# Hybrid decoder block on one core: transfers in program order during attention, weights asked for eight half pieces ahead and in the order of their use

## The chip, the cores and the metric

The kernel runs on one core of a Trainium2 chip. The metric is the device time of one execution in microseconds (us). Five instruction streams work side by side, each strictly in its own order: TensorE (PE, matrix products), VectorE (DVE), ScalarE (ACT), GpSimd (POOL), and SyncE (SP), which here only issues transfers (DMAs). They wait for one another through semaphores. A TensorE clock of 1.00 in the profile is the full 2.4 GHz level; the other level is 1.2 GHz, and a stretch between them is a mean.

## The reference, cut to what matters

One decoder layer on 512 tokens of width 1024, all in float32. Two attention mixers share one normalised input; their gated sum goes through an output projection, and a gated feed-forward of width 2816 follows.

```
proj = rmsnorm(x) @ w_in                       # 1024 -> 4808 columns, split into
qa,ka,va (8 heads of 64), qb (8 heads), kb,vb (one shared head), qi,ki,wi (indexer), ga,gb (gates)
y_a = dilated window attention(rope(qa), rope(ka), va)      # three masks, merged by log-sum-exp
score = sum_h wi_h * relu(rope(qi)_h . rope(ki))            # 512 x 512, causal
y_b = attention(rope(qb), rope(kb), vb) over the 128 best keys of each row of score
x = x + (sigmoid(ga) * (y_a @ w_up_a) + sigmoid(gb) * (y_b @ w_up_b)) @ w_out
x = x + (silu(h @ w_gate) * (h @ w_up)) @ w_down ;  out = rmsnorm(x)
```

## The kernel before

**Products.** Every float32 operand is split in two parts, `hi` (rounded) and `lo` (the rest), and `mm3` makes one product of three matmuls: L201 (hi with hi), L202 and L203 (the two cross terms). Which of L202 and L203 uses the weight's `lo` depends on the side the weights stand on.

**Weights.** A `Chunk` is a block of weight columns, mostly 256 wide, fetched in pieces. `fetch` (L153) asks for one piece by a DMA from SP into one of 5 `raw` buffers. `more` does one half piece at a time: the first call makes `whi` on ACT (L172), and fetches first if nothing was fetched; the second makes `wlo` (L164) on POOL or DVE: in turns before attention, all on POOL during it. There are 8 buffers each for `whi` and `wlo`, that is two chunks of four pieces. If a matmul asks for a piece that isn't there, `Chunk.__getitem__` calls `more` on the spot. `ahead()` takes one half piece of the first unfinished chunk in the list `coming`. It is called 8 times (`LEAD`) before the attention steps. Inside `run_part` it stands behind `if MAN[0]`, and `MAN[0]` is never set, as `DV` is 0. So all later weights are asked for on the spot in the program's text.

**Order of the work.** The kernel is written against a scheduler. Engines in a `manual_schedule` take their instructions in program order; the others get their order at build time from priorities (`level`: attention steps 2, other parts 3, top-k 4), readiness and free buffers, which can move a weight's fetch and split far ahead of its place in the text. Once built, every engine's order is fixed. From L838 to `pe_order.close()`, which is the stage of interest, only PE is manual. Behind it no engine is.

**The stage of interest** in the order of PE's program:
1. Indexer queries and keys are turned (`heads_T`, `idx`), while `P0` makes queries and keys of the first head pair ("slot" products, weights from `qka_parts(0)`). After each slot product `rope_T` copies the result (ACT L488, `raw`), swaps its halves by four DMAs on SP (L491, `sw<-raw`, 64 KB each), and DVE multiplies and adds (L495, L498, L499); then ACT, DVE and POOL make `hi` and `lo` of queries and keys (L422, L426, L441, L442, L446, L447).
2. Scores of the indexer: 24 products (`dots`), each followed by a ReLU on ACT (L861) and a weighted sum on DVE (L866). Between them stand the last half of `P0` and `V0`, the value products of head pairs 0 and 1 ("proj", eight parts; its four pieces are the first chunk of kind `128x2x256`). `V0` isn't in `coming`.
3. 36 attention steps `attn_step(t)`. Step t makes the score products of two heads (`sc`), their softmax (L678 on DVE, exponential L679 on ACT, L683 on DVE, L684 on POOL), and turns the probabilities of the step before (`pT`, L693, L697, L698); every fourth step multiplies by the values (`y`). Between steps, parts of other products are run from a queue: P1, P2 and P3 (head pairs 1 to 3), G0, G1, ... (gates), B (queries and keys of the second mixer), V1. Each part is six matmuls of 512 columns or twelve of 256.
4. The 128 best keys of each score row: 16 rounds of `max` and 15 of `match_replace` (L629, L634) for each of three row blocks, then 18 instructions (L640 to L647) that make the mask. They go to DVE at the lowest priority, and the second mixer needs their result from step 16 on.

The list `order` names the chunks that `ahead()` takes: w1, w2, w3 (of P1 to P3), wkv and wq (of B), wv1 (of V1), wg_ (gates), then those of `w_up_a`.

Of the kernel before, what the change touches and what calls it, by code (L numbers as in the profile page):

```python
# [38 lines left out]
def hybrid_block(ctx: ExitStack, tc: tile.TileContext, x, norm_mix, w_in, w_up_a, w_up_b, w_out,  # L39
# [90 lines left out]
    MAN = [False]  # L130
# [58 lines left out]
    def ahead():  # L189

        while coming and coming[0].done():
            coming.pop(0)
        if coming:
            coming[0].more()
# [142 lines left out]
    def settle(n=1):  # L337
        for _ in range(n):
            for e in later:
                e[0] -= 1  # L340
            while any(e[0] <= 0 for e in later):
                i = next(i for i, e in enumerate(later) if e[0] <= 0)
                later.pop(i)[1]()

    def run_part():
        cost, part = queue.pop(0)
        part()
        settle()
        if MAN[0]:
            ahead()  # L350
        topk_some(TK[2])
        debt[0] -= cost

    def fill(us):

        debt[0] += us
        with level(3):
            while queue and debt[0] > 0:
                run_part()
        if not queue:  # L360
            debt[0] = min(debt[0], 0.0)

    def drain(until=0):
        with level(3):
            while len(queue) > until:
                run_part()
            if not queue:
                settle(9)
        debt[0] = 0.0
# [182 lines left out]
    def va_parts(c):  # L552

        get_w = stream(win, [(VA + 256 * c, 256)])

        def done(p_, b):
            for pr in (2 * c, 2 * c + 1):
                if b == 0:
                    va[pr] = ap.tile([P, NB, 2, P], F32R, tag="va", bufs=VAB, name=f"va{pr}")
                src = p_[:, pr % 2 * P:(pr % 2 + 1) * P].rearrange("p (s d) -> p s d", s=2)  # L560
                vh, vl = va[pr][:, b, :, 0:64], va[pr][:, b, :, 64:128]
                nc.scalar.activation(vh, src, AF.Copy, scale=rs1[:, b:b + 1])
                defer(1, lambda vl=vl, src=src, vh=vh: nc.vector.scalar_tensor_tensor(  # L563
                    vl, src, rs1[:, b:b + 1], vh.bitcast(F32), op0=ALU.mult, op1=ALU.subtract))
        return [proj_parts(get_w, 256, b, lambda p_, b=b: done(p_, b)) for b in range(NB)], get_w
# [11 lines left out]
    def gate_parts(base, c, store):  # L577

        get_w = stream(win, [(base + c * 256, 256)])

        def part(m, k0, p_):
            if k0 == 0:
                p_.append(acc("gate"))
            W = get_w()
            for k in range(k0, k0 + 2):
                l = (W[k][0][:, m * P:(m + 1) * P], W[k][1][:, m * P:(m + 1) * P])
                mm3(p_[0], l, hT[k], k == 0, k == KT - 1)
            if k0 + 2 == KT:
                t = k2(name="gate")
                nc.vector.tensor_tensor(t, p_[0], rb1[0], op=ALU.mult)  # L590
                defer(1, lambda: nc.scalar.activation(t, t, AF.Tanh, scale=0.5))
                store.append(t)
        res = []
        for m in range(2):
            p_ = []
            res.append([(6 * 512 / 2400, lambda m=m, k0=k0, p_=p_: part(m, k0, p_)) for k0 in range(0, KT, 2)])
        return res, get_w

    def flat(*lists):
        return [x for l in lists for x in l]  # L600
# [51 lines left out]
    def topk_some(n):  # L652
        with level(TKL):
            for _ in range(n):
                if topk and next(topk[0], None) is None:
                    topk.clear()
# [179 lines left out]
        weights(2, 8)  # L836
    start.close()
    pe_order = ExitStack()  # L838
    pe_order.enter_context(tc.manual_schedule(engines={mybir.EngineType.PE}))
    nc.sync.dma_start(ropeT, c_ropeT)  # L840
    queue += flat(*second[:NSB])
    drain()
# [38 lines left out]
    V1, wv1 = va_parts(1)  # L881
    B, TV, (*wq, wkv) = mqa_parts(bT)
    G, wg_ = zip(*[gate_parts(base, c, store) for base, store in ((GA, mA), (GB, mB)) for c in range(4)])
# [1 line left out]
    for i, at in enumerate(GAT):  # L885
        seq[at] = seq[at] + flat(*G[i])
    queue += flat(*seq)
    order = [c() for c in (w1, w2, w3, wkv, wv1, *wq, *wg_)]
    for g in G[len(GAT):]:
        queue += flat(*g)  # L890
    yS = []
# [218 lines left out]
```

## Time and profile before

| what | value |
|---|---|
| median of 3 runs (lowest, highest) | 775.24 us (775.01, 775.41) |
| the profiled execution, its own time | 774.55 us |
| its span, first to last instruction | 772.8 us |
| PE busy, share of the span | 744.1 us, 96% |
| DVE, ACT, POOL busy | 435.6, 352.6, 281.4 us |
| mean TensorE clock | 0.993 |
| HBM traffic | 91 GB/s over the span |

Between the span and the time of the profiled execution lie 1.75 us that the trace doesn't show. All other times are read from that one execution, and are counted from the start of the span. A busy PE is not PE at its peak, since matmuls overlap: a 512-column matmul lasts 0.39 us in the trace, but the next begins some 0.23 us after it.

### The profile page before, as it was taken

To read this page: it belongs to the slowest core of one execution; us is meant where nothing else is said; L and a number is where in the kernel's file an instruction comes from. 1 tells how busy PE (TensorE), PEld (TensorE's weight loads), DVE (VectorE), ACT (ScalarE), POOL (GpSimd) and SP (SyncE) were. 2 spreads that over 40 slices of the span, in tenths; PEclk is the share of its full clock that TensorE was granted. 3 is DMA by queue.
4 is the path that set the end of the run, shared out by engine and by line. 5 is a ranking of instruction groups with operands and counts; after the bars stand their busy time and mean duration, and the time that the engine had idled before them with its cause. 6 is when DMAs were issued, how large, how long until landed. Compare 5 with 4: busy or idle time off the path is not lost.

```text
span 772.8 us, 10634 instructions
## 1 busy us (share of the span) xinstructions
PE 744.1 (96%) x3621; PEld 625.2 (81%) x3621; DVE 435.6 (56%) x910; ACT 352.6 (46%) x722; POOL 281.4 (36%) x263
## 2 busy tenths in 40 slices
PE   8988998988999999999999999999999999999995
PEld 7977887886888888888887888888888888888884
DVE  5789989997766557765334344344433343222235
ACT  7366566655666667533425333333333333121233
POOL 2653656645545455422121222222222222222223
PEclk9999999999999999999999999999999999999999
DMA  8352433322432221533232332233223333323202
GB/s 278 80 137 54 102 91 88 89 76 69 117 88 70 73 66 55 176 112 107 82 106 59 109 103 88 83 109 109 84 85 105 109 101 90 105 86 109 83 14 109
DMA packets 68502, 74.53 MB, mean 96 GB/s; under 512 B 5392, under 2 KB 55584, under 8 KB 68448
## 3 DMA queue, kind: packets, MB, share of 16 engines
q1 hardware_dynamic: 68448, 73.86, 32.7%
q8 instruction: 28, 0.46, 0.2%
q14 instruction: 26, 0.21, 0.1%
HBM read 68.46 MB, written 2.10 MB: 91 GB/s over the span
## 4 chain that ended last, share of the span: by engine, by line
PE 82%; DVE 10%; ACT 3%; issue 2%; DMA 1%; SPq 0%; POOL 0%; ACTq 0%; DVEq 0%; POOLq 0%
PE o L202 5%; PE u L203 5%; PE o L203 5%; PE u L202 5%; PE u L201 5%; PE o L201 5%; PE g L203 5%; PE g L202 5%; PE g L201 5%; PE gate L201 3%; PE gate L202 3%; PE gate L203 3%; PE x L203 2%; PE x L201 2%; PE x L202 2%
## 5 line engine op out<-in xcount | busy, mean ns | idle before, releaser
L164 POOL TENSOR_TENSOR wlo<-raw,whi 128x512 fp32r<-128x512 f32 (+1 forms) x156 | 206.1, 1331 | 386.6 <-ACT whi L172 376.4
L172 ACT ACTIVATE whi<-raw 128x512 fp32r<-128x512 f32 (+1 forms) x242 | 149.6, 625 | 240.1 <-PE u L203 70.9
L164 DVE TENSOR_TENSOR wlo<-raw,whi 128x512 fp32r<-128x512 f32 x86 | 71.9, 836 | 128.3 <-ACT whi L172 127.8
L201 PE MATMUL g<-h2h,whi 128*128 128x512 f32 x176 | 68.7, 390 | 0.0
L203 PE MATMUL g<-h2l,whi 128*128 128x512 f32 x176 | 68.7, 390 | 0.0
L202 PE MATMUL g<-h2h,wlo 128*128 128x512 f32 x176 | 68.6, 390 | 0.0
L201 PE MATMUL u<-h2h,whi 128*128 128x512 f32 x176 | 68.5, 389 | 0.0
L202 PE MATMUL u<-h2h,wlo 128*128 128x512 f32 x176 | 68.5, 389 | 0.0
L203 PE MATMUL u<-h2l,whi 128*128 128x512 f32 x176 | 68.5, 389 | 0.0
L201 PE MATMUL o<-whi,ah 128*128 128x512 f32 x176 | 68.5, 389 | 0.0
L202 PE MATMUL o<-whi,al 128*128 128x512 f32 x176 | 68.5, 389 | 0.0
L203 PE MATMUL o<-wlo,ah 128*128 128x512 f32 x176 | 68.5, 389 | 0.0
L684 POOL TENSOR_SCALAR sm<-sm,st 128x256 f32<-128x256 f32 (+3 forms) x64 | 40.0, 632 | 62.4 <-DVE st L683 52.1
L201 PE MATMUL gate<-hTh,whi 128*128 128x512 f32 x128 | 51.6, 403 | 0.0
L203 PE MATMUL gate<-hTl,whi 128*128 128x512 f32 x128 | 50.2, 392 | 0.0
L202 PE MATMUL gate<-hTh,wlo 128*128 128x512 f32 x128 | 50.1, 391 | 0.0
L679 ACT ACTIVATE sm<-sm,st 128x256 f32<-128x256 f32 (+3 forms) x64 | 35.6, 557 | 23.3 <-DVE st L678 23.1
L1025 DVE TENSOR_TENSOR u<-u,rb 128x512 f32<-128x512 f32 x22 | 15.2, 692 | 52.4 <-PE u L203 52.4
L201 PE MATMUL slot<-hTh,whi 128*128 128x512 f32 x104 | 41.7, 401 | 1.8 <-DVE va L563 1.1
L201 PE MATMUL proj<-whi,hTh 128*128 128x256 f32 (+1 forms) x128 | 38.4, 301 | 2.8 <-DVE va L563 1.2
L202 PE MATMUL slot<-hTh,wlo 128*128 128x512 f32 x104 | 40.8, 392 | 0.0
L203 PE MATMUL slot<-hTl,whi 128*128 128x512 f32 x104 | 40.7, 391 | 0.0
(268 smaller groups left out, 1627.0 us busy)
## 6 DMA issues: line engine op xcount, KB each, us to landing
raw<-in_w_in SPq DMA_DIRECT2D x54, 256.0 KB, 3.0
raw<-in_w_gate SPq DMA_DIRECT2D x44, 256.0 KB, 2.9
raw<-in_w_up SPq DMA_DIRECT2D x44, 256.0 KB, 2.9
raw<-in_w_down SPq DMA_DIRECT2D x44, 256.0 KB, 2.8
x<-in_x SPq DMA_DIRECT2D x16, 256.0 KB, 4.0
raw<-in_w_in SPq DMA_DIRECT2D x32, 128.0 KB, 2.5
raw<-in_w_out SPq DMA_DIRECT2D x16, 256.0 KB, 2.6
sw<-raw SPq DMA_DIRECT2D x50, 64.0 KB, 2.0
```

Of the source, the lines that this page charges most:

```text
L164: eng.tensor_tensor(lo, raw, hi.bitcast(F32), op=ALU.subtract)
L172: nc.scalar.activation(hi, raw, AF.Copy)
L201: nc.tensor.matmul(o, l[0], r[0], start=start, stop=False)
L202: nc.tensor.matmul(o, l[1], r[0], start=False, stop=False)
L203: nc.tensor.matmul(o, l[0], r[1], start=False, stop=stop)
L679: nc.scalar.activation(sm, sm, AF.Exp, bias=st[:, 0:1], scale=-1.0, accum_out=st[:, 1:2])
L684: nc.gpsimd.tensor_scalar(sm, sm, st[:, 2:3], 1.0, op0=ALU.mult, op1=ALU.mult)
L1025: nc.vector.tensor_tensor(u, p_, rb2, op=ALU.mult)
```

## The change

Three edits. `run_part` calls `ahead()` after every part, whatever `MAN[0]` is. SP joins PE in the manual schedule, so that from L838 to `pe_order.close()` its DMAs go out in the order of the program's text. And `order` now names the chunks in the order in which the queue uses them.

```
-        if MAN[0]:
-            ahead()
+        ahead()
...
-    pe_order.enter_context(tc.manual_schedule(engines={mybir.EngineType.PE}))
+    pe_order.enter_context(tc.manual_schedule(engines={mybir.EngineType.PE, mybir.EngineType.SP}))
...
-    order = [c() for c in (w1, w2, w3, wkv, wv1, *wq, *wg_)]
+    order = [c() for c in (w1, w2, wg_[0], w3, wg_[1], wkv, wv1, wq[0], wg_[2], wq[1], *wg_[3:])]
```

PE's order stays as it was, row for row. The orders of the other engines change. From L349 on, line numbers after the change are smaller by one.

**SP at the start of the stage.** `128x328` is the last of the indexer's weights, the first `128x2x128` are P0's, the first four `128x2x256` are V0's, the next `128x2x128` are those of P1; `sw<-raw` is the swap of a slot product. Before:

```order
L153 DMA raw<-in_w_in 128x328 x5
L153 DMA raw<-in_w_in 128x2x128 x8
L153 DMA raw<-in_w_in 128x2x256 x4
L153 DMA raw<-in_w_in 128x2x128 x10
L491 DMA sw<-raw 32x512 x4
L153 DMA raw<-in_w_in 128x2x128 x6
L491 DMA sw<-raw 32x512 x4
```

After the change:

```order
L153 DMA raw<-in_w_in 128x328 x6
L153 DMA raw<-in_w_in 128x2x128 x8
L490 DMA sw<-raw 32x512 x4
L848 DMA lc<-in_c_mask 128x512
L490 DMA sw<-raw 32x512 x4
L153 DMA raw<-in_w_in 128x2x256 x4
L153 DMA raw<-in_w_in 128x2x128 x12
L490 DMA sw<-raw 32x512 x4
```

V0's four transfers stood ahead of both swaps of P0 and stand behind both now.

**POOL around attention steps 2 to 4.** `wlo` rows are weights' `lo` halves, `sm` rows are the normalisation L684 of a softmax (two a step), `qk1A..l` rows the keys' `lo` halves. Before, `wlo_1642`, `wlo_1655`, `wlo_1668` and `wlo_1681` are the four pieces of P3; `sm_1438` and `sm_1442` belong to step 2, `sm_1528` and `sm_1532` to step 3:

```order
L684 TENSOR_SCALAR sm_1340<-sm_1340,st_1341 128x384
L164 TENSOR_TENSOR wlo_1642<-raw_1638,whi_1641 128x512
L684 TENSOR_SCALAR sm_1438<-sm_1438,st_1439 128x256
L684 TENSOR_SCALAR sm_1442<-sm_1442,st_1443 128x512
L164 TENSOR_TENSOR wlo_1655<-raw_1651,whi_1654 128x512
L164 TENSOR_TENSOR wlo_1668<-raw_1664,whi_1667 128x512
L446 TENSOR_TENSOR qk1A10l_1327<-z_1316,qk1A10h_1325 64x512
L446 TENSOR_TENSOR qk1A11l_1328<-z_1316,qk1A11h_1326 64x512
L164 TENSOR_TENSOR wlo_1681<-raw_1677,whi_1680 128x512
L684 TENSOR_SCALAR sm_1528<-sm_1528,st_1529 128x128
```

After the change P3's pieces are `wlo_1532`, `wlo_1583`, `wlo_1606` and `wlo_1625`; `sm_1547` and `sm_1551` belong to step 3, `sm_1633` and `sm_1637` to step 4:

```order
L683 TENSOR_SCALAR sm_1551<-sm_1551,st_1552 128x384
L164 TENSOR_TENSOR wlo_1447<-raw_1444,whi_1446 128x512
L164 TENSOR_TENSOR wlo_1489<-raw_1486,whi_1488 128x512
L164 TENSOR_TENSOR wlo_1532<-raw_1528,whi_1531 128x512
L164 TENSOR_TENSOR wlo_1583<-raw_1579,whi_1582 128x512
L683 TENSOR_SCALAR sm_1633<-sm_1633,st_1634 128x512
L683 TENSOR_SCALAR sm_1637<-sm_1637,st_1638 128x256
L445 TENSOR_TENSOR qk1A20l_1510<-z_1499,qk1A20h_1508 64x512
L445 TENSOR_TENSOR qk1A21l_1511<-z_1499,qk1A21h_1509 64x512
L164 TENSOR_TENSOR wlo_1606<-raw_1602,whi_1605 128x512
L164 TENSOR_TENSOR wlo_1625<-raw_1621,whi_1624 128x512
```

P3's third and fourth piece were split before the softmax of step 3 and are split after that of step 4 and the keys that follow it. PE's program uses them between the score products of steps 4 and 5, in both kernels.

**DVE between the gates of G0 and the softmax of step 5.** `max` and `match_replace` are the top-k. Before:

```order
L590 TENSOR_TENSOR gate<-gate,rb_543 128x512 x2
L629 MAX top_1086<-cur_1087 128x8
L629 MAX top_1088<-cur_1089 128x8
L634 MATCH_REPLACE cur_1085<-top_1084,cur_1085 128x512
L678 ISA sm,st<-sc,lc 128x384
```

After the change, from behind the same two gate rows:

```order
L633 MATCH_REPLACE cur_1085<-top_1084,cur_1085 128x512
L633 MATCH_REPLACE cur_1087<-top_1086,cur_1087 128x384
L633 MATCH_REPLACE cur_1089<-top_1088,cur_1089 128x256
L628 MAX top_1084<-cur_1085 128x8
L628 MAX top_1086<-cur_1087 128x8
L628 MAX top_1088<-cur_1089 128x8
L633 MATCH_REPLACE cur_1085<-top_1084,cur_1085 128x512
L633 MATCH_REPLACE cur_1087<-top_1086,cur_1087 128x384
L633 MATCH_REPLACE cur_1089<-top_1088,cur_1089 128x256
L628 MAX top_1084<-cur_1085 128x8
L628 MAX top_1086<-cur_1087 128x8
L677 ISA sm,st<-sc,lc 128x384
```

Eleven top-k instructions stand here where three stood. Counted from the start of the program, 33 maxima precede the second softmax of step 5 before, and 47 of all 48 after the change; the mask is finished around step 10 before, and by the softmax of step 7 after.

## Rows read from the trace of the kernel before

**Rows 1.** Stretches: us from:to, length, busy us (instructions) by engine, clock, DMA share, GB/s.
```profile
50.90:86.20 35.30, 31.25 (x185) 28.07 (x184) 33.96 (x70) 22.36 (x49) 15.48 (x13) 0.95 0.28 68
86.20:152.00 65.80, 63.29 (x305) 52.32 (x304) 62.10 (x171) 40.78 (x83) 40.91 (x35) 1.00 0.38 97
152.00:186.30 34.30, 29.76 (x185) 25.87 (x183) 33.32 (x81) 18.20 (x45) 17.64 (x16) 1.00 0.26 68
...
186.00:200.00 14.00, 12.51 (x56) 10.65 (x57) 9.36 (x24) 9.43 (x23) 7.30 (x8) 0.88 0.41 112
200.00:300.00 100.00, 100.00 (x521) 84.64 (x520) 62.12 (x168) 65.02 (x158) 51.74 (x58) 1.00 0.26 72
```

**Rows 2.** PE's waits, 84 to 190 us: who was waited for, total us, times, longest.
```profile
PE pT L693 <- POOL sm L684: 1.9, 3, 1.5
PE sc L613 <- DVE st L678: 1.4, 1, 1.4
```

**Rows 3.** PE's waits, 40 to 84 us.
```profile
PE dots L613 <- ACT relu L861: 3.8, 3, 1.8
PE idx L468 <- DVE idx0l L434: 1.6, 1, 1.6
PE idx L468 <- POOL z L516: 0.8, 1, 0.8
```

**Rows 4.** Timeline of SP's issues, 38 to 70 us: start, length, instruction, count.
```profile
39.86 9.46 SPq L153 DMA_DIRECT2D raw<-in_w_in  x13
50.28 2.50 SPq L491 DMA_DIRECT2D sw<-raw  x4
...
62.42 3.44 SPq L491 DMA_DIRECT2D sw<-raw  x4
```

**Rows 5.** Timeline of PE around V0's first use.
```profile
63.95 0.41 PE L201 MATMUL proj<-whi,hTh 128*128 128x256 f32 x1
...
68.50 0.52 PE L613 MATMUL dots<-idx0h,idx 128*128 128x384 f32 x2
```

**Rows 6.** Timeline of ACT beside V0.
```profile
69.24 0.87 ACT L861 ACTIVATE relu<-dots 128x384 f32<-128x384 f32 x2 [0.17 <-PE dots L613]
...
71.75 0.62 ACT L441 ACTIVATE qk1A00h<-z 64x512 fp32r<-64x512 f32 x1
```

**Rows 7.** DMA issues: KB each, median us from issue to landing.
```profile
raw<-in_w_in SPq DMA_DIRECT2D x54, 256.0 KB, 3.0
...
sw<-raw SPq DMA_DIRECT2D x50, 64.0 KB, 2.0
```

**Rows 8.** The page's costliest groups: busy us, mean ns of one; idle before, releaser.
```profile
L164 POOL TENSOR_TENSOR wlo<-raw,whi 128x512 fp32r<-128x512 f32 (+1 forms) x156 | 206.1, 1331 | 386.6 <-ACT whi L172 376.4
L172 ACT ACTIVATE whi<-raw 128x512 fp32r<-128x512 f32 (+1 forms) x242 | 149.6, 625 | 240.1 <-PE u L203 70.9
```

**Rows 9.** Timeline of POOL around step 4.
```profile
124.95 1.14 POOL L684 TENSOR_SCALAR sm<-sm,st 128x512 f32<-128x512 f32 x1 [0.83 <-DVE st L683]
126.05 1.69 POOL L164 TENSOR_TENSOR wlo<-raw,whi 128x512 fp32r<-128x512 f32 x1
127.73 0.47 POOL L684 TENSOR_SCALAR sm<-sm,st 128x256 f32<-128x256 f32 x1
128.17 1.27 POOL L446 TENSOR_TENSOR qk1A20l<-z,qk1A20h 64x512 fp32r<-64x512 f32 x1
```

**Rows 10.** Timeline of PE: P3's first slot product, then the score products of step 5.
```profile
118.76 0.39 PE L201 MATMUL slot<-hTh,whi 128*128 128x512 f32 x1
...
121.49 0.39 PE L201 MATMUL slot<-hTh,whi 128*128 128x512 f32 x1
...
124.21 0.33 PE L613 MATMUL sc<-qk1A10h,qk0A 128*128 128x384 f32 x1
```

**Rows 11.** Groups of DVE, 86.2 to 152 us.
```profile
L629 DVE MAX8 top<-cur 128x8 f32<-128x512 f32 (+2 forms) x33 | 16.9, 544 | 0.0
L634 DVE MATCH_REPLACE8 cur<-top,cur 128x512 f32<-128x512 f32 (+2 forms) x31 | 16.7, 543 | 0.0
```

**Rows 12.** A further stretch, columns as in the first group.
```profile
60.00:72.00 12.00, 10.14 (x63) 9.84 (x64) 11.67 (x21) 7.52 (x18) 2.33 (x2) 0.86 0.28 67
```

**Rows 13.** The mask's tile `eq` on DVE alone: stretch, length, busy (instructions).
```profile
152.00:186.30 34.30, 14.37 (x15) 1.00 0.26 68
```

## The prediction

> **What bounds the kernel now.** I read the stretches first. PE does matmuls for 63.29 of 65.80 us between 86.2 and 152, for 29.76 of 34.30 up to 186.3, and for all of 200 to 300 [rows 1]: PE's own order is the bound, and what can change is the time in which PE stands still. That is 65.80 - 63.29 = 2.5 us, 34.30 - 29.76 = 4.5 us and, from 186 to 200, 14.00 - 12.51 = 1.5 us, 8.5 in all, beside 4.0 between 50.9 and 86.2. Second, the waits say for whom. Ahead of the attention steps PE waits 1.6 and 0.8 us for the turned indexer tensors and 3.8 us for ReLUs on ACT [rows 3]; later for the softmax on DVE (longest 1.4) and its normalisation on POOL (1.9 in three) [rows 2]. No wait for a weight is among these rows: fetching and splitting run ahead of PE, and a change of their order can only help by letting DVE, ACT and POOL serve the softmax sooner, and hurt by making a weight late. Third, DVE is busy 62.10 of 65.80 us from 86.2 to 152 and 33.32 of 34.30 after it [rows 1]. So DVE has 3.7 us to spare in the first stretch, and whatever is put in front of a softmax there delays it by nearly its whole length. Fourth, the order of instructions, which names what stands ahead of what at two places: V0, and P3's third piece.
>
> **What costs nothing by itself.** The calls of `ahead()` add no instruction; the numbers of splits and transfers stay as they are, 156 `wlo` of 1.33 us on POOL and 242 `whi` of 0.63 us on ACT [rows 8]. From 200 us on PE is never idle [rows 1], so the later chunks may come earlier or later without a price while they keep ahead of PE; if they don't, one late piece costs what V0 is costed at below. The swaps of P1 to P3 gain in that fewer fetches stand in front of them; I give that nothing.
>
> **V0 comes late.** Before, V0's four fetches stand ahead of both swaps, in a run of 13 issues that begins at 39.86 and lasts 9.46 us (0.73 each) [rows 4], long before V0's first matmul at 63.95 [rows 5]. After, they stand behind both, and V0 isn't in `coming`, so its splits also start only then.
> - What PE gains ahead of V0: the splits of V0 and w1 no longer stand between the indexer's instructions. I count the waits of 1.6 and 0.8 and some 2.1 of the 3.8 [rows 3], 4.5 us. The second swap, issued at 62.42, then starts at 57.9. Its four issues took 2.50 at the first swap and 3.44 at the second [rows 4]; with 2.9, V0's first fetch starts at 60.8.
> - A weight lands 3.0 us after its issue [rows 7]: 63.8 for the first piece, 3 x 0.73 = 2.2 later, 66.0, for the fourth. Split by 0.63 + 1.33 [rows 8], the first piece is ready at 65.8, and PE can begin the first half of V0.
> - The second half needs pieces three and four. On ACT their `whi` stand behind the six key copies (0.62 each) and two pairs of ReLUs (0.87 a pair) [rows 6], and between these copies POOL makes two key differences of 1.27 [rows 9]. From the second `whi` (ending at about 65.7) that is 4 x 0.62 = 2.5 us of copies, to 68.2; the rest of the two differences, to about 69.5; then two more copies, whose POOL partner has to finish, with a pair of ReLUs, to some 70.5; `whi` 71.1, `wlo` 72.4. The last twelve matmuls take about a third of the 4.55 us between the rows 63.95 and 68.50 [rows 5], of which 1.2 remain behind the last `wlo`: V0 ends at 73.6, where it ended at 68.50. **Plus 5 us.** Lower end: ACT doesn't hold anything up, the fourth piece is split at 66.0 + 0.63 + 1.33 = 68.0, the end is at 69.2, +0.7. Upper end: one more pair of ReLUs and both pieces' `wlo` behind each other (0.87 + 1.33) with the slower swap, +8. I take the middle, since the copies stand in ACT's order for certain and only their starts are an estimate.
>
> What the move of V0's fetches costs by itself is told by the rows: an issue at 39.86 has 24 us until 63.95, one at 60.8 has none, and a landing of 3.0 is bare. The Trainium skill ("DMA: Bandwidth & Descriptors", Rules for kernel authors) advises to issue a transfer early, compute, and wait on its semaphore late, so that its fixed setup cost overlaps. The trace of before agrees with it: no wait for a fetch is seen where fetches lead. By that rule alone, one landing of 3.0 us is what V0 loses, and the kernel would come out as in the first rival.
>
> **P3's third piece comes late.** Before, all of P3's first three `wlo` are split ahead of the softmax of step 3 or just behind it. After, the third and fourth stand on POOL behind the normalisation of step 4 and two key differences. That normalisation starts at 124.95 now; with V0's 5 us and two more top-k instructions in front of it (0.54 each [rows 11]) it starts at 131. Behind it: 1.14 + 0.47 + 1.27 + 1.27 (the second difference is costed as the first) [rows 9], to 135.2; the third `wlo` 1.33 [rows 8], to 136.5. PE's first slot product of P3 with the third piece stands at 121.49 now, and its first matmul with that piece's `lo` some 0.23 later [rows 10], so after V0's 5 us at 126.7. **Plus 10 us.** What is behind the waiting matmul is everything of PE: the score products of step 5, at 124.21 now [rows 10], would come at 139. Lower end: POOL waits less for step 4 because its softmax isn't delayed (the 6 us vanish): 5; below that, nothing, if that wait isn't there at all. Upper end: 13, if the pair of `wlo` meets what stretched one from 1.33 to 1.69 at 126.05 [rows 9] and the key differences' copies on ACT come late as well.
>
> DVE says the same from its side. 47 maxima stand before the second softmax of step 5 where 33 stood, and about as many more replacements: 28 x 0.54 = 15 us [rows 11], less some 2.4 to 3.7 of idle time that they fill [rows 1], 11 to 13 us. A PE that waits 10 us for POOL beside it hides this top-k; the two are not summed.
>
> **What comes back.** The mask (14.37 us of DVE in its tile `eq` alone [rows 13]) and the last maxima lie in 152 to 186 now. If they are done earlier, DVE serves each later softmax at once, and the 8.5 us of PE's idle time [rows 1] can go. A part of the first 2.5 lies ahead of P3, and the change of stage at 186 keeps some: **minus 7**, between -5 and -8.5.
>
> **The clock.** PE's clock is 0.86 in 60 to 72 [rows 12] and 0.88 in 186 to 200 [rows 1], 12 x 0.14 = 1.7 and 14 x 0.12 = 1.7 us, both after PE stood still. After the change the second may go, and a new one behind P3's wait comes: 0, between -1.7 and +1.7.
>
> **Sum**: +5 + 10 - 7 = +8. The profiled execution took 774.55, so 782.6; the median of before is 775.24, 0.7 above it, so **783**. The ends of all terms together would be 774.55 + 0.7 + 0 - 8.5 - 1.7 = 765 and 774.55 + 8 + 13 - 5 + 1.7 = 792.
>
> **Rivals.** A measurement of this kernel tells a change of some 0.2%, 1.55 us, from none.
> 1. *Faster.* P3's third piece is ready when PE comes to it, because POOL runs its splits into the gaps it has (it is busy 40.78 of 65.80 us [rows 1]) and the softmax of step 4 is not late; only V0 is exposed, by its landing of 3.0. Then 775.2 + 3.0 - 8.5 = 770. For it: no weight is waited for now, and POOL is idle a third of the time. Against it: POOL is strictly in order, and what stands in front of the piece waits for DVE, which has no time to spare. It decides if the third `wlo` ends by 128, where I put 136.5: up to 5 us late the change still gains. Chance 0.13.
> 2. *No difference.* V0 costs 5, P3's piece is 2 to 3 late, 7 to 8 comes back: 775. Chance 0.07.
> 3. *DVE becomes the longer bound.* Top-k and mask both lie ahead of the softmax of step 7, so PE waits for DVE beyond what P3 costs: from the second softmax of step 5 at +12 the mask's tile adds 14.37 [rows 13], while PE brings 8 to 9 of slack from the parts between the steps, together +17.7 at step 7, of which 7.7 come back: 785. For it: DVE's 62.10 of 65.80 [rows 1]. Against it: what is done early on DVE is missing later, so it is time moved, not added. Chance 0.2.
> 4. *A fetch is late once more*, behind the swaps of P1 to P3, for a chunk of the gates or of B: landing, `whi` and `wlo`, 3.0 + 0.63 + 1.33 = 5 more, 788. For it: SP is strictly in order now, and a swap waits for PE's slot product. Against it: eight half pieces of lead are four pieces, more than these 5 us of PE's work. Chance 0.1.
>
> **How the numbers follow.** The forecast has 0.5. Its own range is 778 to 788 (V0 3 to 8, P3 8 to 12). Faster by over 0.2% is the first rival, 0.14 with a trace of others; within it 0.07; slower 0.79. The range for 8 in 10 takes in rivals 2 to 4 and the upper end of most terms, and leaves out the first rival and a sum of all upper ends: 773.5 to 790.
>
> **What would show it.** V0: PE's `proj` rows wait for `whi` or `wlo` between 59 and 72, ACT's key copies stand ahead of V0's third `whi`, and SP's swap is issued near 58. P3: one wait of about 10 us of a `slot` matmul for POOL's `wlo`, ending near 136, and the score products of step 5 near 139. What comes back: no waits for DVE or POOL from step 7 on, and the mask done by about 170. Wrong would be the forecast if PE's slot products of P3 don't wait (the first rival), if the long wait is one for the softmax on DVE (the third), or if a matmul of G1 or B waits for a weight (the fourth).

## The result and the profile after

The change makes the kernel **slower: 795.36 us median against 775.33, ratio 1.0258 (95% interval 1.0241 to 1.0276)**, 20 us more. The direction was forecast, the size wasn't: 783, with 773.5 to 790 as the range. The two profiled executions, from which everything below is read, took 796.13 and 774.55, 21.6 apart.

The stretches of after, to be held against [rows 1, 12] (from:to, length, busy us with instructions of PE, PEld, DVE, ACT and POOL, granted clock, DMA share, GB/s):

```profile
50.90:86.20 35.30, 25.16 (x124) 21.72 (x123) 31.80 (x59) 19.85 (x42) 12.33 (x10) 0.81 0.37 96
86.20:152.00 65.80, 53.47 (x234) 42.97 (x233) 61.64 (x168) 31.96 (x65) 30.41 (x27) 0.90 0.26 65
152.00:186.30 34.30, 32.32 (x155) 26.86 (x155) 30.00 (x65) 20.56 (x45) 17.66 (x16) 0.95 0.28 77
186.00:200.00 14.00, 14.00 (x114) 13.77 (x113) 9.86 (x23) 9.97 (x26) 9.90 (x10) 0.99 0.43 124
200.00:300.00 100.00, 99.09 (x510) 83.42 (x509) 61.26 (x155) 60.00 (x144) 53.64 (x57) 1.00 0.34 93
60.00:72.00 12.00, 4.80 (x16) 3.85 (x16) 11.26 (x22) 6.47 (x13) 4.07 (x3) 0.72 0.65 175
```

PE now stands still for 12.3 us between 86.2 and 152, where it stood for 2.5, and in the same stretch its clock is 0.90, where it was 1.00. There are two losses: time without a matmul, and matmuls that are slower. From 186 on PE is all but full again. PE's waits from 40 to 200 us (who was waited for, total us, times, longest), beside [rows 2, 3]:

```profile
PE proj L201 <- ACT whi L172: 7.3, 2, 5.1
PE gate L201 <- ACT whi L172: 3.7, 1, 3.7
PE slot L201 <- ACT whi L172: 3.4, 1, 3.4
PE slot L202 <- POOL wlo L164: 3.2, 2, 2.3
PE gate L202 <- POOL wlo L164: 2.0, 2, 1.6
PE pT L692 <- DVE ptl L697: 2.0, 2, 1.7
PE proj L203 <- POOL wlo L164: 1.5, 2, 0.9
```

Six of the seven are waits for a weight's split, of which there was none before: V0 ("proj"), the gate G0, and P2 and P3 ("slot"). Where they stand on PE:

```profile
65.02 0.58 PE L201 MATMUL proj<-whi,hTh 128*128 128x256 f32 x1 [5.08 <-ACT whi L172]
...
72.66 0.39 PE L201 MATMUL proj<-whi,hTh 128*128 128x256 f32 x1 [2.19 <-ACT whi L172]
...
108.21 0.79 PE L202 MATMUL slot<-hTh,wlo 128*128 128x512 f32 x1 [2.25 <-POOL wlo L164]
119.56 0.50 PE L202 MATMUL gate<-hTh,wlo 128*128 128x512 f32 x1 [0.47 <-POOL wlo L164]
127.27 0.50 PE L201 MATMUL gate<-hTh,whi 128*128 128x512 f32 x1 [3.68 <-ACT whi L172]
129.32 0.79 PE L202 MATMUL gate<-hTh,wlo 128*128 128x512 f32 x1 [1.56 <-POOL wlo L164]
147.58 0.51 PE L201 MATMUL slot<-hTh,whi 128*128 128x512 f32 x1 [3.45 <-ACT whi L172]
149.00 0.79 PE L202 MATMUL slot<-hTh,wlo 128*128 128x512 f32 x1 [0.91 <-POOL wlo L164]
```

PE's order is the same in both kernels, so the same instruction can be subtracted. The score products of a step start later than before by:

| score products of step | start before, us | later after the change by | what stands ahead of it |
|---|---|---|---|
| 0 | 85.41 | +9.07 | V0 |
| 2 | 100.29 | +13.26 | P2's third piece |
| 4 | 116.23 | +22.48 | G0 |
| 5 | 124.21 | +28.85 | P3 |
| 9 | 163.81 | +28.08 | |
| 12 | 198.67 | +20.14 | PE's waits for DVE in before are used up |

Four places lose 28.9 us, 8.7 come back. Of the loss, 21.5 us are the waits for weights (9.2 at V0: 5.08, 2.19, 0.56, 0.91 and 0.45; 12.3 in the last six rows above), and V0's start was 4.2 earlier (PE's last scores ahead of V0 end at 59.94, before at 64.15). The remaining 11.6 are matmuls that take longer behind the waits, most of it by the lower clock: G0's thirty, from 127.27 to 138.88, take 11.6 us, where they took 7.1 (109.30 to 116.40), though only 1.56 of the difference is a wait. Their rows start 0.43 us apart first and 0.23 later:

```profile
130.34 0.63 PE L201 MATMUL gate<-hTh,whi 128*128 128x512 f32 x1
130.77 0.63 PE L202 MATMUL gate<-hTh,wlo 128*128 128x512 f32 x1
...
135.51 0.40 PE L202 MATMUL gate<-hTh,wlo 128*128 128x512 f32 x1
135.74 0.39 PE L203 MATMUL gate<-hTl,whi 128*128 128x512 f32 x1
```

What the clock alone took is an estimate. Up to 152, PE was busy at the lower level for 22.0 us of the trace, before for 3.3; half of the difference is 9.4 us. The rest, some 2 us, isn't shown apart; what fits it is that the first matmul behind each of the eleven waits has none in front of it to overlap with (129.32 lasts 0.79 us, the rows behind it 0.63).

Between steps 17 and 18 another 1.4 us are lost; from there the delay stays at 21.5.

Why the weights are late, SP's own waits show. Of after, 40 to 130 us:

```profile
SPq L490 <- ACT raw L487: 55.9, 4, 23.4
SPq L490 <- ACT pth L696: 8.4, 1, 8.4
```

Of before:

```profile
SPq L153 <- POOL wlo L164: 41.3, 21, 14.7
SPq L153 <- POOL z L516: 14.1, 1, 14.1
```

SP waits most of the time in both. Before, it waits in front of a fetch, mostly because no raw buffer is free: it is ahead. After, it waits in front of a swap (L490) whose source hasn't been copied, and all fetches behind that swap wait with it. The longest of these waits, 23.4, ends at P0's first swap, at 49.25; the one at P1's queries lasts 20.5. SP's timeline of after:

```profile
58.78 2.41 SPq L490 DMA_DIRECT2D sw<-raw  x4
61.23 17.19 SPq L153 DMA_DIRECT2D raw<-in_w_in  x16
99.04 2.41 SPq L490 DMA_DIRECT2D sw<-raw  x4
101.55 2.10 SPq L153 DMA_DIRECT2D raw<-in_w_in  x4
103.75 2.41 SPq L490 DMA_DIRECT2D sw<-raw  x4
106.26 1.07 SPq L153 DMA_DIRECT2D raw<-in_w_in  x2
113.06 2.41 SPq L490 DMA_DIRECT2D sw<-raw  x4
115.58 1.07 SPq L153 DMA_DIRECT2D raw<-in_w_in  x2
...
127.37 6.38 SPq L153 DMA_DIRECT2D raw<-in_w_in  x10
```

Between 78.4 and 99.0 nothing is issued. SP stands at the swap of P1's queries, whose source is the copy of P1's first slot product. PE ends that product at 96.5 (its last row starts at 96.07 and lasts 0.39), so nearly all of the wait is the product's place in the program. The copy then stands for 2 us more behind a table load and an exponential on ACT:

```profile
96.42 1.28 ACT L678 ACT_TABLE_LOAD   x1 [4.35 <-DVE st L677]
97.71 0.72 ACT L678 ACTIVATE sm<-sm,st 128x512 f32<-128x512 f32 x1
...
98.44 0.58 ACT L487 ACTIVATE raw<-slot 128x512 f32<-128x512 f32 x1
...
104.78 0.63 ACT L172 ACTIVATE whi<-raw 128x512 fp32r<-128x512 f32 x1 [0.25 <-DMA raw<-in_w_in]
```

Two pieces of P2 are among the 16 issues at 61.23. Its third is issued at 101.55, its `whi` begins at 104.78, and PE comes to need its `lo` before POOL has it (the wait of 2.25 that ends at 108.21). Eight half pieces ahead are four pieces in the text; on SP, swaps take most of that lead.

A late landing is only half of it. V0's first half and P2's third piece do wait for one: their `whi` begins as soon as the fetch is in. But V0's fourth piece had landed at 67.2 us, and the third and fourth were split from 71.98 on. G0's third piece, the first of the two issues at 115.58, was in by about 119 (an estimate: with the 3.3 us that this size takes in the median of this run) and was split at 126.60; P3's third, among the ten at 127.37, was in by 134.1 and was split at 146.92. These splits stand on ACT behind copies of keys:

```profile
123.72 0.63 ACT L446 ACTIVATE qk1A11l<-qk1A11l 64x512 fp32r<-64x512 f32 x1 [1.06 <-POOL qk1A11l L445]
...
126.60 0.62 ACT L172 ACTIVATE whi<-raw 128x512 fp32r<-128x512 f32 x1
...
145.73 0.63 ACT L446 ACTIVATE qk1A21l<-qk1A21l 64x512 fp32r<-64x512 f32 x1 [0.51 <-POOL qk1A21l L445]
146.38 0.63 ACT L590 ACTIVATE gate<-gate 128x512 f32<-128x512 f32 x1
146.92 0.61 ACT L172 ACTIVATE whi<-raw 128x512 fp32r<-128x512 f32 x1
```

There PE waits for ACT's order, which was fixed when the kernel was built.

### The profile page after: what moved, and what is told of

Read it like the earlier page. It is cut to its first block, busy times and chain, and to the rows that moved or that the text cites. A ratio compares the mean times of both kernels' runs of the same rounds, so it can differ in the third digit from the quotient of the medians.

```text
span 794.4 us, 10604 instructions
## 1 busy us (share of the span) xinstructions
PE 754.2 (95%) x3621; PEld 631.8 (80%) x3621; DVE 440.8 (55%) x910; ACT 353.2 (44%) x722; POOL 280.4 (35%) x263
## 4 chain that ended last, share of the span: by engine, by line
PE 74%; DVE 3%; issue 2%; POOL 1%; ACT 1%; POOLq 0%; ACTq 0%; DVEq 0%
PE o L202 5%; PE o L201 5%; PE u L202 5%; PE u L203 5%; PE u L201 5%; PE o L203 5%; PE g L203 5%; PE g L202 5%; PE g L201 5%; PE gate L201 2%; PE gate L202 2%; PE gate L203 2%; PE x L201 2%; PE x L203 2%; PE x L202 2%
## 5 line engine op out<-in xcount | busy, mean ns | idle before, releaser
L164 DVE TENSOR_TENSOR wlo<-raw,whi 128x512 fp32r<-128x512 f32 x86 | 71.1, 827 | 127.8 <-ACT whi L172 127.3
L202 PE MATMUL slot<-hTh,wlo 128*128 128x512 f32 x104 | 42.6, 410 | 3.2 <-POOL wlo L164 3.2
L1024 DVE TENSOR_TENSOR u<-u,rb 128x512 f32<-128x512 f32 x22 | 15.2, 692 | 52.4 <-PE u L203 52.4
```

Of the source, the lines that this page charges most:

```text
L164: eng.tensor_tensor(lo, raw, hi.bitcast(F32), op=ALU.subtract)
L202: nc.tensor.matmul(o, l[1], r[0], start=False, stop=False)
L1024: nc.vector.tensor_tensor(u, p_, rb2, op=ALU.mult)
```

## Experiments

Theory A: SP's program order makes the loss, since fetches stand behind swaps that wait. Rival B: the orders of DVE and POOL (top-k earlier, splits later) make it, wherever a fetch stands. Each run's ratio is to the kernel before on the same chip.

**One part alone: SP in program order.**

```
-engines={mybir.EngineType.PE}
+engines={mybir.EngineType.PE, mybir.EngineType.SP}
```

> One part of the change alone: SP in program order, nothing asked for ahead inside attention, old list. Theory A (SP's order is the cost: a fetch stands behind swaps that wait for PE and ACT, and is late): worse than the full change, since every fetch after P1's also comes without any lead; about 5 us of landing and splitting for each of some eight later chunks beside V0's 9: 810 to 840 us. Rival B (the cost is in the order of DVE and POOL, early top-k and late splits, which the calls of ahead() bring about): SP's order alone costs only V0, 782 to 786.

Measured 845.1 us, 1.0899 (1.0878 to 1.0920): far from B, and 5 us beyond A's range, which was too low. PE waits 27.9 us for `whi` of gates in five waits. The other two parts, in the full change, win back 50 us of what SP's order costs.

**The other two parts, without SP's order.**

```
-        if MAN[0]:
-            ahead()
+        ahead()
...
-    order = [c() for c in (w1, w2, w3, wkv, wv1, *wq, *wg_)]
+    order = [c() for c in (w1, w2, wg_[0], w3, wg_[1], wkv, wv1, wq[0], wg_[2], wq[1], *wg_[3:])]
```

> The other two parts without SP's order: a half piece asked for after every part, chunks in the order of use, SP's transfers placed by the scheduler. Theory A: V0 is fetched ahead of the swaps again, and no weight is late: 770 to 778 us. Rival B: POOL and DVE are still held up, 784 to 796.

Measured 774.9 us, 1.0003 (0.9989 to 1.0017): no difference. The step delays stay at 1.5 us up to step 11 and are 0.0 from step 12. This is what A said; B's 784 to 796 is out. Asking ahead, with the list in order of use, is worth nothing here as long as the scheduler places the fetches, and does no harm.

**V0's fetches ahead of the swaps.** The full change, and in front of the indexer's and P0's products P0's pieces are split and V0's are fetched:

```
+    while not w0().done():
+        w0().more()
+    for _ in range(4):
+        wv0().fetch()
```

> The full change, with P0's four pieces split and V0's four fetches put in the text ahead of P0's products, so that they go out before both swaps. Theory A: PE's wait at V0 (7.3 us for whi, and its clock at half speed behind it) goes, the later lateness of P2, G0 and P3 stays: 785 to 788 us. Rival A2 (the later lateness is a consequence of V0's): all goes, 770 to 778. Rival B: V0's 9 us go as under A, so this run does not tell it from A.

Measured 796.6 us, 1.0271 (1.0255 to 1.0286): nothing gained, against all three theories. Step 0 is delayed by 2.6 us instead of 9.1, so V0 is mended. P2, G0 and P3 still add 4.8, 8.3 and 8.0 (steps 2, 4 and 5), so their lateness is no consequence of V0's. But what is won at V0 is lost, most of it between steps 9 and 11. There ACT, of that run, shows the same chain as above in one piece:

```profile
184.27 0.72 ACT L678 ACTIVATE sm<-sm,st 128x512 f32<-128x512 f32 x1 [6.74 <-DVE st L677]
...
185.49 0.57 ACT L487 ACTIVATE raw<-slot 128x512 f32<-128x512 f32 x1
...
190.41 0.63 ACT L172 ACTIVATE whi<-raw 128x512 fp32r<-128x512 f32 x1 [2.74 <-DMA raw<-in_w_in]
```

and SP, of the same run:

```profile
186.09 1.15 SPq L490 DMA_DIRECT2D sw<-raw  x2
187.33 5.50 SPq L153 DMA_DIRECT2D raw<-in_w_in  x6
```

DVE, busy with the mask up to 183.5, lets ACT wait 6.74 us; so the copy, the swap, the fetch and the `whi` are late one after the other, and this `whi` holds ACT's next exponentials and copies. PE pays 4.12 us at 197.63, in front of a slot product that waits for `va` on DVE.

**Twelve half pieces of lead instead of eight** (`LEAD = 12` in the full change).

> The full change with twelve half pieces of lead instead of eight. Theory A: the pieces of P2, G0 and P3 are asked for six pieces ahead, two more than now, so their waits (about 20 us of delay in the trace after the change) mostly go, V0's 9 us stay: 778 to 783 us. Rival B (POOL and DVE are held up whatever the lead): within 3 us of the full change, 792 to 798.

Measured 791.05 us, 1.0199 (1.0182 to 1.0215), between the theories: 4 us gained. Up to step 4 the delay is a constant 7.7 us, so P2 and G0 are no longer late, as A says; P3 adds 8.6, steps 8 to 11 add 7.1 (below), and step 12 stands at +15.2.

**Swaps issued by ACT** (full change; SP holds only fetches).

```
-            nc.sync.dma_start(sw[32 * i:32 * i + 32, :], raw[o:o + 32, :])
+            nc.scalar.dma_start(sw[32 * i:32 * i + 32, :], raw[o:o + 32, :])
```

> The full change, with the four DMAs of each swap issued by ACT behind the copy that they read, instead of by SP; SP then holds only fetches, still in program order. Theory A (a fetch is late because it stands on SP behind a swap that waits): V0, P2, G0 and P3 are fetched early again and the waits go, 770 to 782 us, with some us of ACT's time for the issues. Rival B (splits stand too late on ACT and POOL, and top-k too early on DVE, wherever the fetch is): 788 to 796.

Measured 782.6 us, 1.0091 (1.0070 to 1.0111). PE waits, 40 to 200 us:

```profile
PE slot L201 <- DVE va L562: 5.7, 2, 3.0
PE gate L201 <- DVE gate L589: 3.3, 1, 3.3
PE proj L201 <- DVE gate L589: 2.8, 1, 2.8
PE dots L612 <- ACT relu L860: 2.4, 3, 1.1
```

No wait for a weight is left at the head of the list. The number alone lies 0.6 us above what A allowed; its pair below compares it with the other order of SP.

**Up to four pieces fetched on top** (full change; splits stay where they are in the text).

```
     if coming:
         coming[0].more()
+    out = sum(len(c.fetched) for c in coming)
+    for c in coming:
+        while out < 4 and len(c.res) + c.per * len(c.fetched) < c.kts:
+            c.fetch()
+            out += 1
```

> The full change, and behind every half piece up to four pieces of the coming chunks are fetched on top (all five raw buffers in use); splits stay where the text has them. Theory A: the fetches of P2's third piece, G0 and P3 no longer lack time, only V0 is late as in the full change, 9 us of which some is won back: 778 to 786 us. Rival B: splits come no earlier, within 3 us of the full change, 792 to 798. Another way to fail: a fetch that waits for a raw buffer holds a swap behind it, then above 798.

Measured 787.2 us, 1.0154 (1.0130 to 1.0177): closer to A, 1 us outside it. Steps 0 to 5 stand at 8.8 us, V0's alone.

**Both: V0's fetches early, four pieces fetched on top.**

> Both the earlier fetches of V0 and four pieces fetched on top. Theory A: no weight is late, 772 to 778 us. Rival B: 788 to 796.

Measured 780.5 us, 1.0061 (1.0038 to 1.0084): 2.5 us above A's range, but 15 of the 20 us are gone, and steps 0 to 5 stand at 2.2. PE's waits of this run, 40 to 200 us (its line numbers are higher by five):

```profile
PE slot L206 <- DVE gate L594: 4.4, 1, 4.4
PE slot L206 <- DVE va L567: 3.9, 1, 3.9
PE proj L206 <- DVE va L567: 3.4, 2, 2.9
```

All three are for DVE: the longest waits that are left are for no fetch.

**Twelve half pieces and V0's fetches early.**

> Twelve half pieces of lead and V0's fetches ahead of both swaps. In the run with twelve half pieces the steps 1 to 5 stood at a constant delay of 7.7 us, which came from V0, and 8.6 were added at P3 alone. Theory A: the 7.7 go and P3's lateness stays in part, 780 to 786 us. Rival (DVE with its mask is the longer bound at step 12, so that V0's gain is lost again as in the run with V0 alone): 788 to 792.

Measured 785.0 us, 1.0115 (1.0084 to 1.0146). Steps 0 to 3 stand at -0.3 to -0.1, step 5 at +11.3 (P3), step 12 at +10.3. The run lies inside A's range; P3 isn't helped by the lead.

**Less top-k.** In the next three runs 4 of 16 rounds are done (`range(4)`, the threshold in column 31), so that DVE has some 39 us less to do.

> The kernel before with 4 of 16 rounds of top-k, 72 instructions of 0.54 us or some 39 us of DVE's work left out (it keeps 32 keys, not 128). PE's waits for DVE and POOL between 86 and 200 us, 8.5 us, go: 766 to 770 us. It is the base for the next two.

> The full change with 4 of 16 rounds of top-k. If late fetches behind the swaps alone make the loss, it stays: 15 to 25 us above the shortened kernel before, 783 to 793. If DVE's top-k in front of the softmaxes makes most of it, at most 6 us above, up to 775.

> The full change with V0's fetches ahead of the swaps, four pieces fetched on top, and 4 of 16 rounds of top-k. If what was left of the loss in the run with all rounds (5 us) was DVE's order, it goes: within 2 us of the shortened kernel before, 766 to 771. If fetches are still late, 772 to 776.

Measured 770.2, 792.7 and 772.6 us. The first is 0.2 us above its range. With DVE relieved, the full change still costs 22.5 us, more than without that: DVE's part of rival B falls as the cause of the main loss. The version with early fetches is 2.3 us above its base, where with all rounds it is 5.1 above its own: some 3 us of those 5 were DVE's top-k. Its 772.6 lies in the range set for fetches that are still late; the rest is there at step 0 already (+3.3 against +0.5 of the shortened kernel before), where PE waits 2.8 us for `va` on DVE and for no weight.

Top-k on DVE also explains why the runs above gain less in time than at their first steps. With all rounds, each of those that fetch earlier (V0 early, twelve half pieces, four on top, and their pairs) loses 3 to 7 us more between steps 8 and 11 (12.7 to 19.8 with twelve half pieces); the full change loses nothing there (25.3 to 24.8), nor does early fetching with 4 rounds (6.4 to 2.6). So fetches that come earlier uncover DVE's top-k as the next bound.

**Swaps on ACT, SP left to the scheduler.**

> A candidate, all rounds of top-k: a half piece after every part and the order of use, SP left to the scheduler, swaps issued by ACT. No fetch waits for a swap and no swap for a fetch; but ACT pays for its issues, and DVE is full in both: 772 to 779 us. Faster than before only if swaps were late on SP in the kernel before, up to 3 us.

Measured 781.6 us, 1.0109 (1.0075 to 1.0142), 2.6 us above its range and 7 us slower than with the swaps on SP. With the runs above it makes a square:

| swaps issued by | SP left to the scheduler | SP in program order |
|---|---|---|
| SP | 774.9 | 795.4 |
| ACT | 781.6 | 782.6 |

SP's program order costs 20.5 us when swaps and fetches share SP, and 1.0 when they don't (20.1 and 0.3, if each run is held against the kernel before on its own chip; 1.0 is inside the noise). That is theory A in one number. The 7 us between the two left cells are what it costs to move the issues to ACT; by what way isn't shown.

No run beats the kernel before except those that leave work out.

## Why the prediction was right in direction and wrong in size

- **V0: forecast +5, measured +9.1.** The start was right (the swap at 58.78, forecast 57.9; first half from 65.02, forecast 65.8; 4.2 us gained ahead, forecast 4.5). The end was 77.39, forecast 73.6: the third piece's `whi` let PE on at 72.66, where 71.1 was forecast, PE then waited 0.91 and 0.45 more for `lo` halves, and the last twelve matmuls ran at the lower clock, a term that had been set to 0.
- **P3: forecast +10 by POOL's normalise and key differences, measured +6.4.** The third and fourth piece do stand on POOL behind them, at 147.66. But what they wait for isn't on POOL: the third piece's `whi` at 146.92 stands on ACT behind the six key copies and a gate's activation, and PE's longer wait there is for ACT (3.45). The place was right, the engine wasn't. (The term's lower end, 5, should have been 4: 10 less the 6 us that vanish.)
- **P2 and G0: forecast nothing, measured +4.2 and +9.2. This is the step that failed**: "the later chunks may come earlier or later without a price while they keep ahead of PE". They don't keep ahead. The fourth rival named the cause, a fetch behind the swaps of P1 to P3, but was given 0.1, one place and 5 us, on the argument that four pieces of lead are more than 5 us of PE's work. The lead is counted in the text; SP held a swap's wait of 20.5 us in front of P2's third piece, and waits of 5.7 and 8.4 in front of G0's third and of P3's. The prediction had looked at what SP carries ahead of V0 and not at every later swap, though the order of SP's instructions showed each.
- **The clock: forecast 0, measured about +9** by the estimate above. These us are part of what V0, P2, G0 and P3 measured, not a fifth loss. The working counted two dips, not what each wait drags behind it.
- **What comes back: forecast -7, measured -8.7** by step 12, and -7.3 from step 18 on. Right.
- **The rivals.** "Faster" and "no difference" fell. DVE as the longer bound holds only behind the fetches: with them mended, some 3 of the remaining 5 us are its top-k.

Where the Trainium skill ("DMA: Bandwidth & Descriptors", Rules for kernel authors) says to issue early and wait late, the runs agree in direction: fetching earlier took 15 us off. One bare landing of 3.0 us, which is V0's price by that rule in the prediction, was far too little (9.1 measured): the page's rule speaks of setup cost, and here the wait of the instruction in front was the price.

**What stays open.** The scheduler makes ACT's and POOL's order from where it expects a fetch, so each experiment that moves fetches also moves splits. That late fetches and the splits ordered after them make the loss is shown. The trace tells where PE waited for a landing (V0's first half, P2) and where for a `whi` that stands too far back on ACT (V0's second half, G0, P3); no run moves one of the two without the other. The share of the lower clock is an estimate from the trace, not from a run. Why the run without SP's order, whose weights are early too, loses nothing between steps 8 and 11 (1.6 to 1.5) isn't shown either.

## What to carry to other kernels

A queue in program order passes each wait on to everything behind it: before fixing an order, list for each transfer what it waits for, and don't let prefetches stand behind a transfer that waits for a product. A lead counted in pieces of the text is only as long as the queue lets it be; read it as the time between the issue and the first use. Where a build fixes every engine's order, a late fetch also moves the work that follows it, so look at where the split stands and not only at when the data landed. And price a wait of several us on TensorE with the slower matmuls behind it: here about half as much again (11.6 on 21.5).

## What the runs showed of the hardware

TensorE's clock was not at its upper level in the stretches behind the waits. From 60 to 72 us, where PE waited 5.08 us for V0, the granted clock was 0.72, a mean between the levels 1.2 and 2.4 GHz; before, with PE's two waits of 1.8 and 1.2 us for ReLUs [rows 3], it was 0.86 [rows 12]. Behind G0's waits 512-column matmuls started 0.43 us apart, and 0.23 apart later. In all, 11.6 us of slower matmuls stood against 21.5 us of waits for weights, about 9 of them by the clock (an estimate). Moving the swaps' issues to ACT cost 7 us in this kernel (774.9 to 781.6), though they landed about as fast as from SP: 2.1 us against 2.0.
